# The first input of a two-layer trunk: transposed raw, in four blocks between the first weights, with its norm applied to the products

## The chip, the cores and the metric

One Trainium2 chip, one of its cores. The metric is the device time of one execution in microseconds (us); lower is better. The kernel before has a median of 2629.19 us over three runs (2629.15 to 2630.71). TensorE is called PE here, VectorE DVE, ScalarE ACT, GpSimd POOL and SyncE SP, as the profile does.

## The reference

Two layers over 256 tokens of 2048 channels, in float32: a gated DeltaNet mixer and then an attention over picked tokens, each followed by a squared-ReLU MLP. Each part starts with an RMS norm. What matters here is the beginning:

```
def rms_norm(x, g):
    y = xf * lax.rsqrt(jnp.mean(xf * xf, axis=-1, keepdims=True) + EPS)
    return y * g
...
u = rms_norm(h, norm_mix[0])            # h is the input x, [256, 2048]
proj = u @ w_in                         # [2048, 12352]: q, k, v, z, b, a
qkv = silu(causal_conv(qkv, conv_w))
beta = sigmoid(b); g = -exp(a_log) * softplus(a + dt_bias)
o = chunk_gated_delta_rule(l2norm(q), l2norm(k), v, g, beta)
o = rms_norm(o, out_norm) * silu(z)
h = h + o @ w_out
h = h + square(relu(rms_norm(h) @ w_up)) @ w_down
```

The norm multiplies each token (a row of x) by one number, 1/sqrt(mean + eps), and each channel by a gain. The number of the token can as well be applied to the product `proj`, token by token. The convolution, its SiLU, the sigmoid, the softplus and the SiLU of z come after it.

## The kernel before

**Products.** All large products run on PE as three products of float32r parts: each operand a is split into `hi` (a rounded copy) and `lo` (the rest), and hi·hi + hi·lo + lo·hi is summed (`mm3`). `x` stands transposed, [128 channels, 256 tokens] for each of 16 blocks k of 128 channels, as `xhi` and `xlo`. The weights come through `Stream`: a tile `raw` of 128 x 1024 is loaded by SP, ACT writes `whi` (a cast), DVE writes `wlo` (raw minus whi). There are four buffers each for `raw`, `whi` and `wlo`; an item of the first layer holds two blocks k. The split runs three items ahead of the products, so the cast of item i+3 can only start when PE has finished with item i-1.

**Order.** Nothing is scheduled behind the program's back: each engine runs its instructions in the order in which the Python code emits them. `Pace` keeps a rough account of when each engine will be free, and `Background` uses it to emit the steps of side chains (generators) between the blocks of the main work: `tick` emits those that should be due, `ensure` emits steps until a named result is there. `by_channel` and `by_token` are the two loops of products; `by_channel` calls `ensure` for block k + `ahead` before it emits the products of block k.

**DMA.** A load that SP or ACT issues signals one of eight completion semaphores, handed out in turn; an issue that reuses one waits until the load before on it has landed, and everything behind it on that engine waits as well.

**The start** (lines 384 to 452). SP loads x in four quarters, then the identity `ident` (part of the tile `wide`), then eight small vectors of gains into `rows`, then the first weights. ACT and DVE square the quarters (`junk`), DVE sums and takes the reciprocal root (`rsqrt`, ten small steps), PE transposes `rows` into `vecs`, and `normalise(c)` scales 512 columns of x. The generator `first` transposes a block of x on PE (two matmuls with `ident` into a bank `aux`) and splits it into `xhi` (ACT) and `xlo` (DVE), with the gain of the channel. Two blocks are emitted ahead; then group 0 of the projections starts with `ahead=3`: 16 blocks, 12 products each, into two banks `acc`.

**Layer 0** (lines 454 to 725). After group 0 come the products of b and a (48), the chain `decays` (DVE, ACT, then a transpose of the tile `E` on PE), and the products of z (`zo`). For each of 16 groups of two heads, ACT copies the four products of [128, 256] into `s`, and the chain `delta` does the convolution, the triangular inverse and the output `r`, in the background of the next groups' products.

Of the kernel before, what the change touches and what calls it, by code (L numbers as in the profile page):

```python
# [27 lines left out]
class Pace:  # L28
    """A rough account of when each engine gets through what it has been given, in microseconds."""
# [98 lines left out]
class Stream:  # L128
    """The weights in the order of their use: loaded, and split into two float32r parts, ahead of it."""
# [9 lines left out]

    def get(self):  # L140
# [3 lines left out]
        while self.split < min(i + ahead + 1, len(self.items)) or self.loaded < min(i + self.loads + 1, len(self.items)):  # L144
            while self.loaded < min(self.split + self.loads - self.ahead, len(self.items)):
                (n, w), pieces = self.items[self.loaded]
                raw = self.raw_pool.tile([P, 1024], F32, name="raw")
                view = raw[:, : n * w].rearrange("p (n w) -> p n w", n=n)
                for at, src in pieces:
                    self.sync.dma_start(out=at(view), in_=src)  # L150
                self.raw[self.loaded] = raw
                self.loaded += 1
# [17 lines left out]
def tile_hybrid_trunk(ctx: ExitStack, tc: tile.TileContext, a: dict, out: bass.AP):  # L170
# [38 lines left out]
    QO, KO, VO, ZO, BO = 0, 2048, 4096, 8192, 12288  # L209
    for g in range(DN_G):  # L210
        for k in range(0, KD, 2):
            ws.add((2, 512), [
# [68 lines left out]
    def rsqrt(y, x, n, eng=dve):  # L281
        """y = 1/sqrt(x), elementwise over [P, n]."""
# [14 lines left out]
    def split(src, hi, lo, scale=None):  # L297
        """float32 values in PSUM or SBUF, scaled by the partition, as two float32r parts."""
# [42 lines left out]
    def by_channel(n_items, part, key, n_ct=4, ahead=0):  # L341
        """Channels on partitions: [128 channels, 256 tokens] each, two to a bank."""
# [16 lines left out]
    def by_token(n_items, part, key, n_cols=512, outs=None, k0=0):  # L359
        """Tokens on partitions: [128 tokens, n_cols] for each of the two blocks of tokens."""  # L360
# [17 lines left out]
    def two_chunks(tiles, key, nk):  # L378
        """The first two blocks of columns of a mixer's output, which leave the last heads to the end."""
        outs = [by_token(nk // 2 - 2, h_part(tiles), key) for _ in range(2)]  # L380
        return [by_token(2, h_part(tiles), key, outs=o, k0=nk - 4) for o in outs]

# [1 line left out]
    with tc.tile_pool(name="first", bufs=1) as fp:  # L384
# [3 lines left out]
        quarters = [(tb, slice(c * 1024, c * 1024 + 1024)) for c in range(2) for tb in range(2)]  # L388
        for tb, s in quarters:
            sync.dma_start(out=xin[:, tb, s], in_=a["x"][0, tb * P:tb * P + P, s])  # L390
        sync.dma_start(out=ident, in_=a["consts"][:, 0:P])
        dve.memset(rows, 0.0)
        at = 0
        VEC = {}
        for name, src in (
# [4 lines left out]
            sync.dma_start(out=rows[at:at + n, :], in_=src.rearrange("(n p) -> n p", p=P))  # L400
# [9 lines left out]
        sq4 = small_tile(4, "sq4")  # L410
        for n, (tb, s) in enumerate(quarters):
            junk = fp.tile([P, 1024], F32, name="junk", bufs=2)
            if n % 2 == 0:
                act.activation(junk, xin[:, tb, s], AF.Square, accum_out=sq4[:, n:n + 1])
            else:
                dve.scalar_tensor_tensor(junk, xin[:, tb, s], 1.0, xin[:, tb, s], op0=OP.mult, op1=OP.mult, accum_out=sq4[:, n:n + 1])
        rs = small_tile(2, "rs")
        sq = small_tile(2, "sq")
        dve.tensor_tensor(sq, sq4[:, 0:2], sq4[:, 2:4], op=OP.add)
        dve.tensor_scalar(sq, sq, 1.0 / D, EPS, op0=OP.mult, op1=OP.add)  # L420
        rsqrt(rs, sq, 2)
# [4 lines left out]
        def normalise(c):  # L426
            s = slice(c * 512, c * 512 + 512)
            act.activation(xin[:, 0, s], xin[:, 0, s], AF.Copy, scale=rs[:, 0:1])
            dve.tensor_scalar(xin[:, 1, s], xin[:, 1, s], rs[:, 1:2], None, op0=OP.mult)

        normalise(0)

        def first():
            for k in range(KD):
# [5 lines left out]
                if k % 4 == 1 and k < 12:  # L440
                    normalise(k // 4 + 1)
                yield
            t = aux()
            for i in range(2):
                pe.transpose(t[:, i * P:i * P + P], cwr[:, i, :], ident)
            act.copy(cw, t[:, 0:T])

# [3 lines left out]
        first_banks = by_channel(8, x_part, "x0", ahead=3)  # L451
        bg.drain()

# [1 line left out]
    tokc = const.tile([P, 2, P], F32, name="tokc")  # L455
    GLM, BETA, GL = 32, 64, 96
    hT = []
    with tc.tile_pool(name="delta", bufs=2, reuse_waits="tile") as dp:
        gl_dram = dramp.tile([DN_H, T], F32, name="gl_dram")

        def decays(ps):
# [6 lines left out]
            act.activation(ba[64:96], ps[64:96, :T], AF.Tanh, scale=0.5)  # L468
# [3 lines left out]
            dve.tensor_scalar(xa, ps[q, :T], par[q, 1:2], None, op0=OP.add)  # L472
# [28 lines left out]
        def delta(g, s, zg):  # L501
# [86 lines left out]
            # (1 + L)^-1 by doubling its diagonal blocks. L^T is la[b][:, i, 0]; of the four matrices the blocks of 32 are  # L588
            # held apart, T in Tc and T^T in Tct, until they are put together in Tt
# [58 lines left out]
            # y = T r, with what the first block takes from the second's r  # L648
# [17 lines left out]
            # o, its norm and its gate  # L666
# [21 lines left out]
            pool.tensor_tensor(pair(f), pair(f), rep(sc), op=OP.mult)  # L688
            yield True
# [13 lines left out]
        for g in range(DN_G):  # L703
# [4 lines left out]
            for c in range(2):  # L708
                act.copy(s[:, 2 * c:2 * c + 2].rearrange("p n t -> p (n t)"), banks[c])
# [6 lines left out]
            for b in range(2):  # L716
                act.activation(zg[:, b], zo[b], AF.Tanh, scale=0.5)
# [8 lines left out]

    spare[:] = [None, "pk0", None, "pk1"]

# [6 lines left out]
    def chunk_done(outs, c, key, gain, scale=None, last=True):  # L735
        """A block of 512 columns of the residual stream; where it is final, what the next layer takes."""
# [62 lines left out]
    with tc.tile_pool(name="dsa", bufs=1, reuse_waits="tile") as sp, ExitStack() as late:  # L799
# [15 lines left out]
        def q_latent():  # L815
            # 1/sqrt(mean(q^2) + eps) of q = rstd*u is rsqrt(mean(u^2) + eps/rstd^2)/rstd
# [228 lines left out]
```

## Time and profile before

| what | value |
|---|---|
| median of three runs | 2629.19 us (2629.15 to 2630.71) |
| span of the profiled execution (first to last instruction) | 2626.4 us |
| its own device time | not listed apart; the fastest run is 2629.15 us, 2.8 us above the span |
| PE busy | 2588.8 us, 99% |
| DVE, ACT, POOL busy | 1546.4 us (59%), 1292.3 us (49%), 331.1 us (13%) |
| first x transpose, first product, third product | 15.15, 18.38, 19.64 us |
| DMA | 455.95 MB, mean 174 GB/s |

Busy time is the union of an engine's instructions; a matmul's end is modelled, so neighbouring matmuls overlap in the rows, and the step from one start to the next says more than the duration. "Line 78" is the helper through which every compute instruction is emitted, so tiles, not lines, tell what an instruction is. Times are counted from the span's start. A wait names what ended last before the instruction; where that engine had long been done, it was another, often a DMA.

### The profile page before, as it was taken

The page shows a single profiled execution, that of the slowest core. Times are in us where ns is not written, and L with a number is a line of the kernel's source. Part 1 is how long each engine was busy: PE and PEld are TensorE (multiplying, and loading weights), DVE is VectorE, ACT ScalarE, POOL GpSimd, SP SyncE. Part 2 cuts the span into 40 slices and gives each one's busy share as a digit, 9 for nine tenths or more (in the row PEclk, how much of TensorE's full clock was granted, in tenths as well). Part 3 has the DMA queues.
Part 4 walks back from the last instruction along what each step waited for, and adds up shares of the span by engine and source line. Part 5 has one row for each costly group of instructions (what it writes and reads, how often), then busy time and mean ns, then how long its engine had stood idle before and what let it go on. Part 6 is the DMA issues. An engine that isn't in the chain of part 4 may idle for free.

```text
span 2626.4 us, 52946 instructions
## 1 busy us (share of the span) xinstructions
PE 2588.8 (99%) x21827; PEld 2362.0 (90%) x21827; DVE 1546.4 (59%) x2313; ACT 1292.3 (49%) x1995; POOL 331.1 (13%) x674
## 2 busy tenths in 40 slices
PE   7999999999999999999999999999999999999997
PEld 7999999999987899988899988898899988999886
DVE  5777676676764555554455554586555544455544
ACT  4555555555554444443344444566544433444443
POOL 0344444343431000000000000000000000000000
PEclk9999999999999999999999999999999999999999
DMA  6655455555554566666666666643666666666664
GB/s 191 186 147 141 137 150 139 149 146 147 144 168 153 182 189 195 194 193 193 193 186 186 190 190 188 181 133 120 179 191 194 193 195 194 189 188 187 192 193 137
DMA packets 325394, 455.95 MB, mean 174 GB/s; under 512 B 18280, under 2 KB 159840, under 8 KB 324768
## 3 DMA queue, kind: packets, MB, share of 16 engines
q1 hardware_dynamic: 321888, 443.85, 56.8%
q10 hardware_dynamic: 2928, 7.37, 0.8%
q8 instruction: 171, 2.80, 0.4%
q0 software_dynamic: 336, 1.34, 0.1%
q14 instruction: 71, 0.58, 0.1%
HBM read 450.37 MB, written 2.13 MB: 172 GB/s over the span
## 4 chain that ended last, share of the span: by engine, by line
PE 66%; DVE 1%; ACT 0%; issue 0%; ACTq 0%; DVEq 0%
PE acc L78 64%; PE aux L78 1%; PE pk L78 1%; DVE wlo L78 0%; DVE score L78 0%; ACT whi L78 0%; DVE p L78 0%; DVE m L78 0%; ACT acc L78 0%; DVE qtl L78 0%; DVE nm L78 0%; ACT h L78 0%; DVE h L78 0%; DVE rs_t L78 0%; DVE rs_u L78 0%
## 5 line engine op out<-in xcount | busy, mean ns | idle before, releaser
L78 DVE TENSOR_TENSOR wlo<-raw,whi 128x1024 fp32r<-128x1024 f32 x842 | 1029.6, 1229 | 868.4 <-ACT whi L78 861.3
L78 ACT CAST whi<-raw 128x1024 fp32r<-128x1024 f32 x842 | 878.3, 1049 | 853.3 <-PE acc L78 820.7
L78 PE MATMUL acc<-whi,h 128*128 128x512 f32 x2816 | 886.0, 392 | 2.1 <-ACT acc L78 2.1
L78 PE MATMUL acc<-xhi,whi 128*128 128x256 f32 x3088 | 875.9, 284 | 0.3 <-ACT whi L78 0.3
L78 PE MATMUL acc<-xhi,wlo 128*128 128x256 f32 x3088 | 860.5, 279 | 0.5 <-DVE wlo L78 0.5
L78 PE MATMUL acc<-xlo,whi 128*128 128x256 f32 x3088 | 860.8, 279 | 0.0
L78 PEld LDWEIGHTS acc<-whi,h 128*128 128x128 f32 x2816 | 528.7, 188 | 112.2 <-ACT acc L78 2.9
L78 PEld LDWEIGHTS acc<-xhi,wlo 128*128 128x128 f32 x3088 | 585.1, 189 | 0.8 <-DVE wlo L78 0.8
L78 PEld LDWEIGHTS acc<-xhi,whi 128*128 128x128 f32 x3088 | 581.3, 188 | 4.6 <-ACT whi L78 0.7
L78 PEld LDWEIGHTS acc<-xlo,whi 128*128 128x128 f32 x3088 | 581.8, 188 | 0.2
L78 PE MATMUL acc<-wlo,h 128*128 128x512 f32 x1408 | 548.3, 389 | 0.0
L78 PEld LDWEIGHTS acc<-wlo,h 128*128 128x128 f32 x1408 | 264.5, 188 | 52.7
L78 PE MATMUL acc<-whi,xhi 128*128 128x256 f32 (+2 forms) x576 | 173.6, 301 | 0.0
L78 PE MATMUL acc<-whi,xlo 128*128 128x256 f32 (+2 forms) x576 | 166.4, 289 | 0.0
L78 PE MATMUL acc<-wlo,xhi 128*128 128x256 f32 (+2 forms) x576 | 166.1, 288 | 0.0
L78 POOL DMA_DIRECT2D gain<-in_norm_final x1 | 0.6, 639 | 973.2 <-issue 973.2
L78 DVE SCALAR_TENSOR_TENSOR y<-s,cw,y 128x255 f32<-128x255 f32 (+2 forms) x192 | 93.8, 489 | 40.5 <-ACT y L78 36.0
L78 POOL TENSOR_SCALAR E<-R,tokc 128x128 f32<-128x128 f32 x96 | 86.3, 911 | 247.6 <-DMA R<-gl_dram 144.7
L78 PEld LDWEIGHTS acc<-whi,xhi 128*128 128x128 f32 x576 | 108.0, 187 | 3.6
L78 POOL TENSOR_TENSOR h<-h,gain 128x512 f32<-128x512 f32 x8 | 10.1, 1283 | 790.5 <-ACT acc L78 790.5
L78 PEld LDWEIGHTS acc<-wlo,xhi 128*128 128x128 f32 x576 | 108.3, 188 | 1.3
L78 PEld LDWEIGHTS acc<-whi,xlo 128*128 128x128 f32 x576 | 108.1, 188 | 1.2
(239 smaller groups left out, 1955.9 us busy)
## 6 DMA issues: line engine op xcount, KB each, us to landing
raw<-in_mlp_w_up SPq DMA_DIRECT2D x256, 512.0 KB, 4.3
raw<-in_mlp_w_down SPq DMA_DIRECT2D x256, 512.0 KB, 4.3
raw<-in_dn_w_in SPq DMA_DIRECT2D x66, 512.0 KB, 4.1
raw<-in_dn_w_in SPq DMA_DIRECT2D x256, 128.0 KB, 2.9
raw<-in_dn_w_in SPq DMA_DIRECT2D x128, 256.0 KB, 3.3
raw<-in_dn_w_out SPq DMA_DIRECT2D x64, 512.0 KB, 3.8
raw<-in_dsa_w_out SPq DMA_DIRECT2D x32, 512.0 KB, 3.7
raw<-in_dsa_w_uq SPq DMA_DIRECT2D x16, 512.0 KB, 4.2
```

What stands on the lines that cost most here:

```text
L78: r = f(*args, **kwargs)
```

## The change

x comes in four blocks of 512 columns for all tokens, each listed as a piece of a weight item (items 0, 2, 4 and 6), so that SP issues it between the weights. The identity and the gains are loaded from ACT's queue. PE begins with ten matmuls of the tile `ones` with itself. `first` transposes and splits raw x; the squares of a block follow its fourth transpose, and after block 15 come the reciprocal root `rs0` [128, 2], two diagonal tiles `dg`, and a matmul of ones with them that writes the root as a row over all partitions, `rs_row` [128, 256]. `by_channel` for group 0 gets `ahead=1`. What was normalised before is now scaled behind the products: `s` (DVE instead of ACT), the two inputs of `decays`, the tanh of z (scale `rs_half`), and one more POOL multiplication in the output's factor `f`.

```
@@ Stream
+    def fetch(self):
+        while self.loaded < min(self.split + self.loads - self.ahead, len(self.items)):
...
@@ the list of weights, group 0
+            block = slice(k * P, k * P + 512)
+            ws.add((2, 512), ([((lambda v, c=block: xin[:, :, c]), x_rows[:, :, block])] if g == 0 and k % 4 == 0 else []) + [
...
@@ the start
-        quarters = [(tb, slice(c * 1024, c * 1024 + 1024)) for c in range(2) for tb in range(2)]
-        for tb, s in quarters:
-            sync.dma_start(out=xin[:, tb, s], in_=a["x"][0, tb * P:tb * P + P, s])
-        sync.dma_start(out=ident, in_=a["consts"][:, 0:P])
+        t = aux()
+        for _ in range(10):
+            pe.matmul(t[:, 0:P], lhsT=ones, rhs=ones, start=True, stop=True)
         dve.memset(rows, 0.0)
+        act.dma_start(out=ident, in_=a["consts"][:, 0:P])
...
-            sync.dma_start(out=rows[at:at + n, :], in_=src.rearrange("(n p) -> n p", p=P))
+            act.dma_start(out=rows[at:at + n, :], in_=src.rearrange("(n p) -> n p", p=P))
...
-        normalise(0)
+        def squares(c):
+            s = slice(c * 512, c * 512 + 512)
+            junk = fp.tile([P, 2, 512], F32, name="junk", bufs=2)
+            act.activation(junk[:, 0], xin[:, 0, s], AF.Square, accum_out=sq8[:, c:c + 1])
+            dve.scalar_tensor_tensor(junk[:, 1], xin[:, 1, s], 1.0, xin[:, 1, s], op0=OP.mult, op1=OP.mult,
+                                     accum_out=sq8[:, 4 + c:5 + c])
@@ first
                 split(t[:, :T], xT[0][:, k], xT[1][:, k], vec("mix0", k))
                 ready.add(("x0", k))
-                if k % 4 == 1 and k < 12:
-                    normalise(k // 4 + 1)
-                yield
+                yield
+                if k % 4 == 3:
+                    squares(k // 4)
+            sq = small_tile(2, "sq")
+            dve.tensor_reduce(sq, sq8.rearrange("p (b c) -> p b c", b=2), axis=AX.X, op=OP.add)
+            dve.tensor_scalar(sq, sq, 1.0 / D, EPS, op0=OP.mult, op1=OP.add)
+            rsqrt(rs0, sq, 2)
+            dg = fp.tile([P, 2, P], F32, name="dg")
+            for tb in range(2):
+                dve.tensor_scalar(dg[:, tb], ident, rs0[:, tb:tb + 1], None, op0=OP.mult)
+            yield
+            t = aux()
+            pe.matmul(t[:, :T], lhsT=ones, rhs=dg.rearrange("p b c -> p (b c)"), start=True, stop=True)
+            act.copy(rs_row, t[:, :T])
+            yield
...
-        first_banks = by_channel(8, x_part, "x0", ahead=3)
+        first_banks = by_channel(8, x_part, "x0", ahead=1)
@@ decays
-            act.activation(ba[64:96], ps[64:96, :T], AF.Tanh, scale=0.5)
+            dve.tensor_tensor(ba[64:96], ps[64:96, :T], rs_row[64:96], op=OP.mult)
+            act.activation(ba[64:96], ba[64:96], AF.Tanh, scale=0.5)
...
-            dve.tensor_scalar(xa, ps[q, :T], par[q, 1:2], None, op0=OP.add)
+            dve.tensor_tensor(xa, ps[q, :T], rs_row[q], op=OP.mult)
+            dve.tensor_scalar(xa, xa, par[q, 1:2], None, op0=OP.add)
@@ delta, the output's factor
+            pool.tensor_tensor(pair(f), pair(f), rep(rs0), op=OP.mult)
@@ the groups
-                act.copy(s[:, 2 * c:2 * c + 2].rearrange("p n t -> p (n t)"), banks[c])
+                dve.tensor_tensor(s[:, 2 * c:2 * c + 2], banks[c].rearrange("p (n t) -> p n t", n=2),
+                                  rs_row.unsqueeze(1).to_broadcast([P, 2, T]), op=OP.mult)
...
-                act.activation(zg[:, b], zo[b], AF.Tanh, scale=0.5)
+                act.activation(zg[:, b], zo[b], AF.Tanh, scale=rs_half[:, b:b + 1])
```

How the order on the engines moves is seen at three places. The first is ACT in the middle of group 0, before: `xhi` is the rounded part of a block of x, `whi` that of a weight item, `xin` the scaling of raw x.

```order
13 L78 CAST whi<-raw 128x1024 x2
14 L78 ACTIVATE xhi<-aux,vecs 128x256 x2
15 L78 CAST whi<-raw 128x1024
16 L78 ACTIVATE xhi<-aux,vecs 128x256
17 L78 ACTIVATE xin<-xin,rs 128x512
18 L78 ACTIVATE xhi<-aux,vecs 128x256
19 L78 CAST whi<-raw 128x1024
20 L78 ACTIVATE xhi<-aux,vecs 128x256 x2
```

The same stretch of ACT in the changed kernel, where `junk` holds the squares:

```order
19 L78 CAST whi<-raw 128x1024 x2
20 L78 ACTIVATE xhi<-aux,vecs 128x256 x2
21 L78 CAST whi<-raw 128x1024
22 L78 ACTIVATE xhi<-aux,vecs 128x256
23 L78 ACTIVATE junk,sq_131<-xin 128x512
24 L78 ACTIVATE xhi<-aux,vecs 128x256
25 L78 CAST whi<-raw 128x1024
26 L78 ACTIVATE xhi<-aux,vecs 128x256 x2
```

The pattern of casts and splits is the same, but counted from the start of the list there stand nine `xhi` ahead of row 15 before (blocks 0 to 8) and seven ahead of row 21 now (blocks 0 to 6). The cast there is that of item 6 in both, so the split of x runs two blocks less ahead of the weights. DVE has the same order with `xlo` and `wlo`.

The second place is the start of PE, first before:

```order
1 L78 MATMUL aux<-wide,rows 128x128
2 L78 MATMUL aux<-wide,xin 128x128 x8
3 L78 MATMUL acc<-xhi,whi 128x256
4 L78 MATMUL acc<-xlo,whi 128x256
5 L78 MATMUL acc<-xhi,wlo 128x256
```

and in the changed kernel:

```order
1 L78 MATMUL aux<-ones 128x128 x10
2 L78 MATMUL aux<-wide,rows 128x128
3 L78 MATMUL aux<-wide,xin 128x128 x4
4 L78 MATMUL acc<-xhi,whi 128x256
5 L78 MATMUL acc<-xlo,whi 128x256
6 L78 MATMUL acc<-xhi,wlo 128x256
```

Ten matmuls on ones stand ahead of everything, and two blocks of x (four transposes) instead of four stand ahead of the first product.

The third place is PE at the end of group 0 in the changed kernel; `dg` is the diagonal tile of the root, `cwr` the raw weights of the convolution, and the products from row 212 on are those of `decays`.

```order
207 L78 MATMUL acc<-xhi,whi 128x256
208 L78 MATMUL acc<-xlo,whi 128x256
209 L78 MATMUL acc<-xhi,wlo 128x256
210 L78 MATMUL aux<-dg,ones 128x256
211 L78 MATMUL aux<-wide,cwr 128x128 x2
212 L78 MATMUL acc<-xhi,whi 128x256
213 L78 MATMUL acc<-xlo,whi 128x256
```

Before, the transposes of `cwr` stand two blocks earlier, between the products of blocks 13 and 14, and no matmul waits for a norm. Now the matmul with `dg` stands behind the last product of group 0 and ahead of all later ones.

## Rows read from the trace of the kernel before

**Rows 1.** The page's span and its first section: busy time of each engine.
```profile
span 2626.4 us, 52946 instructions
PE 2588.8 (99%) x21827; PEld 2362.0 (90%) x21827; DVE 1546.4 (59%) x2313; ACT 1292.3 (49%) x1995; POOL 331.1 (13%) x674
```
**Rows 2.** What PE waited for, whole span: total us, times, longest us.
```profile
PE aux L78 <- DVE sq L78: 12.3, 1, 12.3
PE aux L78 <- ACT xin L78: 2.4, 1, 2.4
PE acc L78 <- ACT acc L78: 2.1, 2, 1.0
...
PE aux L78 <- DVE E L78: 1.5, 1, 1.5
```
**Rows 3.** Timeline of the start: start us, duration us, engine, instruction, idle before.
```profile
11.62 0.08 DVE L78 DVE_READ_ACCUMULATOR junk<-xin 128x1 f32 x1
...
12.31 0.45 PE L78 MATMUL aux<-wide,rows 128*128 128x128 f32 x1 [12.31 <-DVE sq L78]
...
14.18 0.16 DVE L78 SCALAR_TENSOR_TENSOR rs<-rs_u,rs 128x2 f32<-128x2 f32 x1
...
15.15 1.11 PE L78 MATMUL aux<-wide,xin 128*128 128x128 f32 x4 [2.40 <-ACT xin L78]
...
18.38 0.58 PE L78 MATMUL acc<-xhi,whi 128*128 128x256 f32 x1 [0.28 <-ACT whi L78]
...
19.64 0.58 PE L78 MATMUL acc<-xhi,wlo 128*128 128x256 f32 x1 [0.47 <-DVE wlo L78]
```
**Rows 4.** Timeline of the start: the first landing of x, the last small load.
```profile
5.38 1.06 ACT L78 ACTIVATE junk<-xin 128x1024 f32<-128x1024 f32 x1 [3.37 <-DMA xin<-in_x]
...
10.66 0.25 SPq L400 DMA_DIRECT2D rows<-in_dn_out_norm  x1
```
**Rows 5.** Timeline of PE in group 0: steps early and late.
```profile
23.86 0.41 PE L78 MATMUL acc<-xlo,whi 128*128 128x256 f32 x1
24.07 0.41 PE L78 MATMUL acc<-xhi,wlo 128*128 128x256 f32 x1
...
39.22 0.38 PE L78 MATMUL aux<-wide,xin 128*128 128x128 f32 x2
...
40.84 0.38 PE L78 MATMUL aux<-wide,xin 128*128 128x128 f32 x2
```
**Rows 6.** Busy time by stretch: length, engines (instructions), granted clock, DMA share, GB/s.
```profile
15.00:24.30 9.30, 7.69 (x32) 6.49 (x33) 5.16 (x9) 5.87 (x11) 0.00 (x0) 1.00 0.89 243
24.50:46.70 22.20, 22.20 (x195) 22.20 (x195) 15.52 (x22) 14.14 (x23) 0.00 (x0) 1.00 0.71 197
...
77.40:120.00 42.60, 42.19 (x469) 40.91 (x470) 35.60 (x65) 25.54 (x42) 20.68 (x29) 1.00 0.66 183
120.00:740.00 620.00, 619.71 (x8648) 585.10 (x8647) 436.16 (x929) 355.86 (x758) 265.84 (x555) 1.00 0.52 143
```
**Rows 7.** Timeline of PE: first product after group 0; f32 matmuls of 768 columns.
```profile
46.75 0.28 PE L78 MATMUL acc<-xhi,whi 128*128 128x256 f32 x1
...
94.06 1.45 PE L78 MATMUL pk<-s 128*128 128x512 f32 x4
```
**Rows 8.** Timeline of ACT and DVE: a cast, its rest, the next split of x.
```profile
31.22 1.05 ACT L78 CAST whi<-raw 128x1024 fp32r<-128x1024 f32 x1 [0.79 <-PE acc L78]
...
32.30 1.23 DVE L78 TENSOR_TENSOR wlo<-raw,whi 128x1024 fp32r<-128x1024 f32 x1 [0.94 <-ACT whi L78]
33.44 0.48 DVE L78 SCALAR_TENSOR_TENSOR xlo<-aux,vecs,xhi 128x256 fp32r<-128x256 f32 x1
```
**Rows 9.** Groups by form: out, in, count, busy us, mean ns, idle before.
```profile
L78 DVE TENSOR_TENSOR h<-acc,h 128x512 f32<-128x512 f32 x16 | 10.1, 682 | 0.0
...
L78 ACT COPY s<-acc 128x512 f32<-128x512 f32 x26 | 14.1, 591 | 1.3 <-PE acc L78 1.1
```
**Rows 10.** Timeline of PE: the transposes of E in the chain of decays.
```profile
77.45 0.44 PE L78 MATMUL aux<-wide,E 128*128 128x128 f32 x2 [1.49 <-DVE E L78]
```

More of the change, by code (lines that the diff above doesn't have):

```diff
@@ L138, in add @@
         self.items.append((shape, pieces))
+    def fetch(self):
+        while self.loaded < min(self.split + self.loads - self.ahead, len(self.items)):
+            (n, w), pieces = self.items[self.loaded]
+            raw = self.raw_pool.tile([P, 1024], F32, name="raw")
+            view = raw[:, : n * w].rearrange("p (n w) -> p n w", n=n)
+            for at, src in pieces:
+                self.sync.dma_start(out=at(view), in_=src)
+            self.raw[self.loaded] = raw
+            self.loaded += 1
     def get(self):
@@ L144, in get @@
         while self.split < min(i + ahead + 1, len(self.items)) or self.loaded < min(i + self.loads + 1, len(self.items)):
[L145 to L152, printed above, removed]
+            self.fetch()
             if self.split >= min(i + ahead + 1, len(self.items)):
@@ L209, in tile_hybrid_trunk @@
     QO, KO, VO, ZO, BO = 0, 2048, 4096, 8192, 12288
+    x_rows = a["x"][0].rearrange("(b p) d -> p b d", p=P)
     for g in range(DN_G):
         for k in range(0, KD, 2):
-            ws.add((2, 512), [
+            block = slice(k * P, k * P + 512)
+            ws.add((2, 512), ([((lambda v, c=block: xin[:, :, c]), x_rows[:, :, block])] if g == 0 and k % 4 == 0 else []) + [
                 (lambda v: v[:, :, 0:128], w_in[:, k:k + 2, KO + g * 128:KO + g * 128 + 128]),
@@ L381, in two_chunks @@
         return [by_token(2, h_part(tiles), key, outs=o, k0=nk - 4) for o in outs]
+    carry = ExitStack()
+    carried = carry.enter_context(tc.tile_pool(name="carried", bufs=1))
+    tokc = carried.tile([P, 2, P], F32, name="tokc")
+    rs0 = carried.tile([P, 2], F32, name="rs0")
+    rs_half = carried.tile([P, 2], F32, name="rs_half")
+    rs_row = carried.tile([P, T], F32, name="rs_row")
     with tc.tile_pool(name="first", bufs=1) as fp:
@@ L408, in vec @@
             return vecs[:, VEC[name] + i:VEC[name] + i + 1]
[L410 to L421, printed above, removed]
+        sq8 = small_tile(8, "sq8")
+        ws.fetch()
         tp = aux()
@@ L424, in tile_hybrid_trunk @@
         act.copy(vecs, tp[:, 0:72])
-        def normalise(c):
+        def squares(c):
             s = slice(c * 512, c * 512 + 512)
-            act.activation(xin[:, 0, s], xin[:, 0, s], AF.Copy, scale=rs[:, 0:1])
-            dve.tensor_scalar(xin[:, 1, s], xin[:, 1, s], rs[:, 1:2], None, op0=OP.mult)
-        normalise(0)
+            junk = fp.tile([P, 2, 512], F32, name="junk", bufs=2)
+            act.activation(junk[:, 0], xin[:, 0, s], AF.Square, accum_out=sq8[:, c:c + 1])
+            dve.scalar_tensor_tensor(junk[:, 1], xin[:, 1, s], 1.0, xin[:, 1, s], op0=OP.mult, op1=OP.mult,
+                                     accum_out=sq8[:, 4 + c:5 + c])
         def first():
@@ L446, in first @@
             act.copy(cw, t[:, 0:T])
+            ready.add("first")
         bg.add(first())
@@ L450, in tile_hybrid_trunk @@
         bg.step()
-        first_banks = by_channel(8, x_part, "x0", ahead=3)
+        first_banks = by_channel(8, x_part, "x0", ahead=1)
         bg.drain()
-    tokc = const.tile([P, 2, P], F32, name="tokc")
     GLM, BETA, GL = 32, 64, 96
@@ L459, in tile_hybrid_trunk @@
         gl_dram = dramp.tile([DN_H, T], F32, name="gl_dram")
+        dve.tensor_scalar(rs_half, rs0, 0.5, None, op0=OP.mult)
         def decays(ps):
@@ L725, in tile_hybrid_trunk @@
         bg.drain()
+    carry.close()
     spare[:] = [None, "pk0", None, "pk1"]
```

## The prediction, made before the result was known

> **What bounds the kernel now.** I read the page's first section, then the list of what TensorE waited for, then the start of the timeline, then the busy time by stretch. The page says that TensorE (PE) is the bound: it is busy for 2588.8 of 2626.4 us [rows 1]. So a change is worth only what it takes from the 37.6 us in which PE does not work, or what it adds to them. The list of waits shows where these are: 12.3 + 2.4 us lie ahead of the first products, and the next ones are 2.1 us and 1.5 us [rows 2]. Everything that the change can win lies therefore in the first 20 us. What it can lose lies anywhere in layer 0, whose order it alters.
>
> The start goes like this [rows 3]. PE transposes the parameter rows at 12.31, then waits. VectorE (DVE) ends the squares of the raw input at 11.62, takes until 14.34 for the reciprocal root, the first quarter is scaled, PE transposes from 15.15, and the first product starts at 18.38; its third product must wait for `wlo` until 19.64. The first block of x had landed by 5.38, the last small load was issued at 10.66 [rows 4]. So the products start 13 us after the first half MB is there, and that chain is what the change cuts.
>
> From there PE runs without a gap. [...] The 192 products of group 0 end there: the one that starts at 46.75 is the first of the next stage, `decays` [rows 7]. That is the point at which I compare.
>
> **The change part by part.** *The start.* The squares, the root and the scaling no longer stand ahead of the first transposes. What still does: the parameter rows, because the split of x takes its gains from them. They now come from ScalarE's (ACT's) queue, nine issues, of which the last four wait for earlier loads to land. These loads and SP's share eight completion semaphores, so that an issue waits until an earlier load has landed, as the one at 10.66 did before. The trace has no such queue at the start. Bounds for the transpose of the rows: not before x could land, 5.4 [rows 4], and not after its old 12.31. I take 8.2, nearer to 5.4, because SP keeps at most some 0.8 MB in flight instead of 2 MB. From that transpose to the first product it was 0.45 us to its end, and 3.23 from the x transposes to the product, 0.6 of it a scaling that now goes: 8.2 + 0.45 + 2.65 = 11.3. Call this S; it is 7.1 us earlier than 18.38. From the bounds, S lies between 8.5 and 15.4.
>
> *The run after S.* 192 products at 0.1135 are 21.8 us and 14 pairs of transposes at 0.26 are 3.6: 25.4. The third product waits for `wlo` as before: 1.0 us. Then comes a price. `ahead` falls from 3 to 1, so the order puts the transposes of block k+2 between the products of k and k+1. ACT and DVE stay in order: for each pair of blocks the split of the next-but-two weight tile stands between the two splits of x (the order's rows in the part on the change). That `whi` waits until PE has done with its buffer, i.e. until the products of an odd block end. Before, it went: `whi` 31.22, `wlo` 32.30, `xlo` 33.44 to 33.92 [rows 8], 2.7 us from the release to `xlo`, plus 0.1 to PE. Before, three blocks of products lay in that time. Now PE has one pair of transposes, 12 products, another pair and one product: 0.26 + 1.36 + 0.26 + 0.11 = 1.99 us, and then stands for 0.85. This comes at blocks 7, 9, 11, 13 and 15: 4.3 us. At blocks 3 and 5 two weight tiles stand in a row ahead of the split; walking the same durations gives 1.1 and 0.85. Sum of stalls: 6.3 us.
>
> *The end of group 0.* The norm now comes last: after the last `xlo` DVE does the squares of 512 columns (about 0.65, half of the old 1024), the root (2.7 us from 11.62 to 14.34, [rows 3]) and two diagonal tiles (0.4): 3.75 us. PE has 11 products left, 1.25 us, and the matmul of ones with the diagonal stands next in its order, ahead of the whole next stage: 2.5 us of wait. The matmul itself is 256 columns of f32; 768 take 1.45 us [rows 7], so 0.45; with the conv transposes 0.7.
>
> *Clock.* Before, PE stepped at 0.21 for 6.0 us after its first product, though it had been working on and off since 15.15. [...] So I take the low level again until S + 6.0. Slow products cost less than before, since the stalls shrink beneath them (at 0.21 the chain of 2.8 us hides under 12 products of 2.56): walking it, 1.4 us against a start at the high level.
>
> [...]
>
> *Sum to the comparison point:* 11.3 + 25.4 + 1.0 + 6.3 + 2.5 + 0.7 + 1.4 = 48.6, against 46.75: 1.9 us later. A start that is 7 us earlier is spent on 6.3 of new stalls, 3.2 of the late norm, and little else.
>
> *Layer 0 after that.* `s` is now a DVE multiply from PSUM, 0.68 us, where ACT copied in 0.59 [rows 9]: 32 of them, 1.36 us of DVE per group. DVE is busy for 436 of 620 us between 120 and 740, and PE is never idle there; but between 77.4 and 120 DVE is at 84% [rows 6]. I cost this at 0 where cover is 30% and 0.4 us in the dense stretch; the bound above is the whole 1.36 in 15 groups, 20 us, and below nothing, since ACT was not what PE waited for. `decays` has two more DVE steps (about 1 us) ahead of the transposes of E, for which PE waited 1.5 us [rows 10]; these now stand 12 products (1.36 us) later in PE's order: -0.4. One more GpSimd step of four columns per group lies behind other work. Sum 0.
>
> The profile's span is 2626.4; the runs' median of 2629.2 lies 2.8 above it, which I leave as it is, since the change lies inside the span. Forecast: 2629.2 + 1.9 = 2631.1, i.e. **no change that a measurement of this kernel can tell** (0.2%, 5.3 us, is about that bound).
>
> **The rivals.**
> - *The clock is up at S* (the ones do it, or the idle stretch does not undo it). For: ten dense matmuls. Against: the 6 us of [rows 5] after work since 15.15. Time: 2629.7. Chance 22%.
> - *The lost look-ahead costs nothing*, because ACT and DVE run the splits of x before PE needs them. For: before, DVE waited for `whi`, not for work. Against: the in-order chain of 2.7 us in [rows 8]. Then -6.3 us: 2624.8, with the clock up as well 2623.4, the only way past -0.2%. Chance 12%.
> - *DVE becomes the bound in layer 0* (the slower side): `s` stands in DVE's order ahead of the weights' `wlo`, and PE runs out of split weights. It decides once more than about half of the 1.36 us per group is exposed: 0.6 × 15 = 9 us, 2640. For: 84% in the dense stretch. Against: 30% idle later, and `wlo` waits mostly for buffers. Chance 10%.
> - *The rows land no earlier* because of the shared semaphores: S = 15.4, 4.1 us more: 2635.2; from there anything above makes it measurably slower. Chance 11%.
>
> **How the numbers follow.** The forecast has 45%, the rivals the rest. Measurably faster: most of the stall-free case with something else going well, and an S near 8.5 with the clock up (-2.3): 11%. Measurably slower: the DVE case and half of the late-rows case: 16%. The rest, 73%, is within 0.2%. The range goes from the stall-free case, 2624.5, to just beyond the late rows, 2637.
>
> **What would show it.** First product between 9.5 and 13, not 18.4. In group 0, waits of PE for `xlo` of 0.8 to 1.1 us at every second block, about 6 us in all, and one of about 2.5 us for `dg`; if they are missing, the second rival holds. The stage after group 0 starting at 47 to 49. The step of the first products (0.21 or 0.114) tells the clock. PE idle of under 2 us more than before between 60 and 780; if it is 5 or more, with DVE named, the third rival holds. A first product after 14 means the fourth. Wrong is this prediction if the time falls below 2624 or exceeds 2637, or if it falls between them with the start and the stalls both absent.

## The result, and the profile after

The changed kernel takes 2646.74 us (median of 4 runs, 2645.53 to 2648.14), the kernel before 2629.17 (4 runs, 2629.05 to 2630.71). The ratio is 1.0065, 95% interval 1.0051 to 1.0078: it is slower by 0.65%, 17.6 us. The forecast was 2631.1, range 2624.5 to 2637, so the time lies outside the range. The profiled execution has a span of 2646.0 us, 19.6 more than before. It is the slowest of the four (2648.14 us); their mean granted clock goes from 0.995 (this one) to 0.998 (2645.53 us), so what the clock takes in this trace need not come in every execution.

The page's first section, after (answers to [rows 1]):
```profile
span 2646.0 us, 53033 instructions
PE 2610.2 (99%) x21849; PEld 2382.1 (90%) x21849; DVE 1574.4 (60%) x2350; ACT 1279.7 (48%) x1964; POOL 331.8 (13%) x690
```
TensorE (PE) idles for 35.8 us, where it was 37.6. It is the *busy* time that grew, by 21.4 us, for 22 matmul records more (the ten products of ones and the one with `dg`, two records each). Some 4 us of it cost nothing, since the ones run while PE had nothing else to do:
```profile
1.05 4.05 PE L78 MATMUL aux<-ones 128*128 128x128 f32 x20 [1.05 <-DVE ones L78]
```
A share of busy time doesn't say how long a matmul takes.

The list of PE's waits, after (total us, times, longest us; answers to [rows 2, 10]):
```profile
PE acc L78 <- DVE xlo L78: 4.6, 7, 0.9
PE aux L78 <- DMA rows<-in_dn_out_norm: 4.4, 1, 4.4
PE aux L78 <- DVE rs_half L78: 2.3, 1, 2.3
...
PE aux L78 <- DVE E L78: 0.5, 1, 0.5
```
The 12.3 us for `sq` are gone; 4.4 for the parameter rows, 4.6 for `xlo` and 2.3 for the norm (the wait named `rs_half`) have come.

The timeline of PE at the start, after (answers to [rows 3]):
```profile
9.53 0.45 PE L78 MATMUL aux<-wide,rows 128*128 128x128 f32 x1 [4.43 <-DMA rows<-in_dn_out_norm]
9.77 1.21 PE L78 MATMUL aux<-wide,xin 128*128 128x128 f32 x4
12.47 0.58 PE L78 MATMUL acc<-xhi,whi 128*128 128x256 f32 x1 [1.50 <-ACT whi L78]
```
And inside group 0 (answers to [rows 5]):
```profile
28.23 0.38 PE L78 MATMUL aux<-wide,xin 128*128 128x128 f32 x2
28.37 0.36 PE L78 MATMUL acc<-xhi,whi 128*128 128x256 f32 x1
29.43 0.39 PE L78 MATMUL acc<-xlo,whi 128*128 128x256 f32 x1 [0.70 <-DVE xlo L78]
...
30.84 0.38 PE L78 MATMUL aux<-wide,xin 128*128 128x128 f32 x2
32.48 0.38 PE L78 MATMUL aux<-wide,xin 128*128 128x128 f32 x2
```
Between two pairs of transposes lie 2.61 us where `xlo` is awaited (28.23 to 30.84) and 1.64 where it is not (30.84 to 32.48): 0.97 us a stall, near the forecast's walk (0.85). There are five such stalls, one smaller (0.24 us of idle) and, before the last block, one larger (0.90).

The timeline of PE at the end of group 0, after (answers to [rows 7]: the product at 51.52 is the first of `decays`; the one at 59.07 is the first of the gate's, `zo`):
```profile
50.26 1.19 PE L78 MATMUL aux<-dg,ones 128*128 128x256 f32 x2 [2.29 <-DVE rs_half L78]
51.24 0.63 PE L78 MATMUL aux<-wide,cwr 128*128 128x128 f32 x2
51.52 0.56 PE L78 MATMUL acc<-xhi,whi 128*128 128x256 f32 x1
51.88 0.41 PE L78 MATMUL acc<-xlo,whi 128*128 128x256 f32 x1
...
55.66 0.28 PE L78 MATMUL acc<-xlo,whi 128*128 128x256 f32 x1
55.77 0.28 PE L78 MATMUL acc<-xhi,wlo 128*128 128x256 f32 x1
...
59.07 0.28 PE L78 MATMUL acc<-whi,xhi 128*128 128x256 f32 x1
```
After the wait of 2.29 us the clock is at its low level again: the products step at 0.21 us from 51.88 on (granted clock 0.56 in 52:56) and at 0.11 or 0.12 only from 55.66 (1.00 in 56:60). The 48 products of `decays` take 7.55 us (51.52 to 59.07); before, they took 5.44, from 46.75 to the first product of the gate:
```profile
52.19 0.28 PE L78 MATMUL acc<-whi,xhi 128*128 128x256 f32 x1
```

Busy time by stretch, after (length, then busy us and instructions of PE, PEld, DVE, ACT, POOL, then granted clock, DMA share, GB/s; answers to [rows 6]):
```profile
0.00:11.00 11.00, 5.50 (x25) 4.66 (x25) 0.31 (x2) 1.97 (x3) 3.22 (x9) 0.85 0.73 207
11.00:24.00 13.00, 10.83 (x69) 10.34 (x70) 9.28 (x13) 8.56 (x13) 0.00 (x0) 0.73 1.04 317
...
48.00:80.00 32.00, 29.75 (x230) 29.49 (x231) 21.61 (x40) 12.65 (x17) 0.00 (x0) 0.89 0.45 123
...
160.00:760.00 600.00, 600.00 (x8331) 565.07 (x8333) 447.18 (x928) 336.29 (x704) 250.48 (x544) 1.00 0.53 148
```
Here the granted clock shows the level: 0.85 in the first 11 us (it rose near the end of the ones, whose step falls from 0.21 to 0.11 us at about 4.4, and fell again before the first product: it reads 0.50 from 8 to 18 us, where the products step at 0.21), 0.73 in the next stretch, and 0.89 after the wait. In layer 0 PE is busy for 600.00 of 600 us, and the changed kernel doesn't fall further behind there: 6.9 us at the first product of the gate (59.07 against 52.19), 5.5 at the end. The DVE multiplies cost nothing.

I then took the time at which each of the 842 weight tiles is cast, in both traces, and subtracted. The changed kernel is 5.5 us behind when layer 0 ends, 12.3 us behind after the first half of MLP 0 (its 1536 products of the up projection), still 13 at the second MLP's start, and 19.6 after the first up half of MLP 1. So some 13 us are lost in two stretches in which the change alters no instruction. One view shows it: PE's matmuls in 100 us of each of the four up halves (stretch, its length, PE's busy time and count, granted clock, DMA share, GB/s). Before:
```profile
1000.00:1100.00 100.00, 100.00 (x885) 1.00 0.65 200
1350.00:1450.00 100.00, 100.00 (x852) 1.00 0.63 193
1960.00:2060.00 100.00, 100.00 (x885) 1.00 0.65 200
2310.00:2410.00 100.00, 100.00 (x851) 1.00 0.62 194
```
After:
```profile
1000.00:1100.00 100.00, 100.00 (x851) 1.00 0.59 182
1350.00:1450.00 100.00, 100.00 (x852) 1.00 0.61 185
1960.00:2060.00 100.00, 100.00 (x852) 1.00 0.61 188
```
PE is busy for every one of the 100 us, at full clock, in all of them. But before, the first halves run 885 products (113 ns each), the second halves 852 (117.4 ns); after, all run at 117.4. 1536 products × 4.4 ns = 6.7 us a half, 13.5 in all. I call the two levels the 113 and the 118 ns step.

### The profile page after: what moved, and what is told of

It reads as the page before. It is cut to its first block, busy times and chain, and to the rows that moved or that the text cites. A ratio compares the mean times of both kernels' runs of the same rounds, so it can differ in the third digit from the quotient of the medians.

```text
span 2646.0 us, 53033 instructions
## 1 busy us (share of the span) xinstructions
PE 2610.2 (99%) x21849; PEld 2382.1 (90%) x21849; DVE 1574.4 (60%) x2350; ACT 1279.7 (48%) x1964; POOL 331.8 (13%) x690
## 4 chain that ended last, share of the span: by engine, by line
PE 93%; DVE 3%; DMA 1%; ACT 1%; issue 1%; POOL 1%; SPq 0%; ACTq 0%; DVEq 0%; POOLq 0%
PE acc L78 84%; PE aux L78 7%; PE pk L78 2%; DVE wlo L78 2%; DMA raw<-in_dn_w_in 1%; ACT whi L78 1%; DMA R<-gl_dram 0%; DVE y L78 0%; POOL rs_u L78 0%; SPq L146 0%; POOL f L78 0%; DVE score L78 0%; POOL E L78 0%; DMA wide<-in_consts 0%; DVE p L78 0%
```

## Experiments

"a_" is an edit of the changed kernel, "b_" one of the kernel before. Times are medians of 4 to 10 executions in three rounds, beside the kernel before on the same chip (2628.4 to 2630.0), ratios to that with 95% intervals. "Place" means an address in an SBUF partition, given as what it lies over a multiple of 256 bytes. The up projection loads `whi` or `wlo` as the stationary operand and streams `xhi` or `xlo`. Before, the weights' tiles have place 32 and the x tiles 224; in the changed kernel `tokc` has left the constants for a pool of its own, every weight tile lies 896 bytes lower, at place 160, and x stays at 224.

**1. The weights' addresses, put back (a_pad) and taken over (b_shift).**
```diff
-    tokc = carried.tile([P, 2, P], F32, name="tokc")
+    tokc = const.tile([P, 2, P], F32, name="tokc")
...
-        sq8 = small_tile(8, "sq8")
+        sq8 = fp.tile([P, 8], F32, name="sq8")
```


> The changed kernel with two small tiles put elsewhere in SBUF, so that raw, whi, wlo and h have the addresses that they have in the kernel before; no instruction is added or moved. Theory A (the addresses set the product step): the first up half of both MLPs falls from 118 to 113 ns a step, 1536 products x 4.4 ns = 6.7 us each, and the time from 2646.7 to about 2633. Theory B (the step is set by what PE ran before it, not by addresses): both stay at 118 ns and the time within 1 us of 2646.7.

2633.69 us, ratio 1.0018 (1.0009 to 1.0028). Its up halves of MLP 0:
```profile
1000.00:1100.00 100.00, 100.00 (x884) 1.00 0.62 194
1350.00:1450.00 100.00, 100.00 (x852) 1.00 0.59 186
```
The reverse, on the kernel before (`tokc` in a pool that closes after layer 0, 128 bytes of padding, so that the addresses are the changed kernel's):
```diff
-    tokc = const.tile([P, 2, P], F32, name="tokc")
+    carried = carry.enter_context(tc.tile_pool(name="carried", bufs=1))
+    tokc = carried.tile([P, 2, P], F32, name="tokc")
...
+    pad = const.tile([P, 32], F32, name="pad")
```


> The kernel before with tokc put elsewhere, so that raw, whi, wlo and h have the addresses of the changed kernel; no instruction of TensorE is added or moved. Theory A (addresses): the first up half of both MLPs goes from 113 to 118 ns and the time from 2629.2 to about 2642. Theory B (what PE ran before): 113 ns stays, 2629 stays.

2642.14 us, ratio 1.0049 (1.0034 to 1.0064), 852 matmuls in 100 us in the first halves. Theory A holds in both directions and in size: 13.05 us come back (12.7 if each time is set against the kernel before beside it), 13.3 are lost, and PE's instructions are the same. Of the 17.6 us, 13 are where `tokc` lies.

**2. The ones on the kernel before (b_ones).** The ten products are put ahead of its first transpose.

> The kernel before with the ten products of ones ahead of its first transpose and nothing else. Theory B (PE's history sets the step): the step of the first up halves may turn to 118 ns, +6.7 us for each; theory A (addresses): they stay at 113 ns. For the start: the ten products raise the clock to full by about 5 us as in the changed kernel (0.85 granted over 0:11), and it is back at half before the first product at 18.4, so that the start gains nothing: 46.7 for the first decays product, within 0.3 us.

2629.16 us, ratio 1.0001 (0.9991 to 1.0010); 885 matmuls in the first halves. What PE ran at the start doesn't set the step (what it runs just before the products can, see 6), and the ones gain nothing.

**3. The look-ahead (a_ahead3).**
```diff
-        first_banks = by_channel(8, x_part, "x0", ahead=1)
+        first_banks = by_channel(8, x_part, "x0", ahead=3)
```


> The changed kernel with the look-ahead of the transposes at 3 blocks, as before, in place of 1. Theory C (the look-ahead costs its stalls): the PE waits for xlo, 4.6 us over seven places, go to under 0.5, and the first decays product comes 2 to 4.6 us earlier than 51.9; the wait for dg grows by what the chain of the norm doesn't gain. Rival: the wait at dg takes all of it (grows from 2.3 to 6 or more) and the stage ends at 51.9 as now. The MLP step says the rest: 6.7 us for each first up half that turns to 113 ns (theory B allows it, theory A doesn't).

2636.89 us, ratio 1.0030 (1.0019 to 1.0042): 9.85 us less than the changed kernel. Its waits in the first 110 us:
```profile
PE aux L78 <- DMA rows<-in_dn_out_norm: 3.6, 1, 3.6
PE aux L78 <- DVE E L78: 1.5, 1, 1.5
...
PE aux L78 <- DVE dg L78: 0.7, 1, 0.7
PE aux L78 <- DVE xlo L78: 0.6, 1, 0.6
```
and by stretch, as above:
```profile
24.00:48.00 24.00, 23.34 (x198) 23.06 (x198) 17.49 (x40) 12.57 (x21) 0.00 (x0) 1.00 0.65 184
48.00:80.00 32.00, 30.52 (x268) 30.32 (x267) 26.00 (x43) 14.13 (x20) 0.46 (x1) 1.00 0.59 174
```
The first `decays` product comes at 41.57, where it was 51.52: 9.95 us earlier, twice what theory C, which counted the idle time of the stalls alone, expected. The stalls cost 6.5 us with the time lost behind each (five of 0.97; the other two, by the same rows, some 0.5 and 1.2). With the transposes done earlier the norm is done earlier as well, and the wait falls from 2.3 to 0.7 us. The product with `dg` and its transposes take 0.65 us (40.92 to 41.57) in place of 1.26, since the clock stays up: the products behind it step at 0.12 us, and the column says 1.00 in 48:80, where it was 0.89. The rest, some 1.3 us, is in the start: the first product 0.3 us earlier, two pairs of transposes ahead of it and not behind, and the full step from 16.8 us on in place of 18.1. The step in the MLPs is 118 ns as theory A says (852 in 100 us). The rival, that the wait for `dg` eats the gain, is refuted.

**4. The wait for the norm, moved behind `decays` (a_lateg).**
```diff
         first_banks = by_channel(8, x_part, "x0", ahead=1)
+        first_ba = by_channel(2, x_part, "x0", n_ct=1)[0]
         bg.drain()
...
-                bg.add(decays(by_channel(2, x_part, "x0", n_ct=1)[0]))
+                bg.add(decays(first_ba))
```


> The changed kernel with the 48 decays products emitted ahead of the wait for the norm: the product of ones with dg now comes near the end of them in place of ahead of them. Theory D (the wait for dg costs twice, once as idle 2.3 us and once more as 6.8 us in which the clock is at half, some 3.4 us): the wait for dg goes, the clock stays full from 18 us on, and the time falls by 5 to 6 us, to about 2641. Rival (the drop of the clock comes from the product of ones in fp32 or from the stalls on xlo, not from this wait): only 2.3 us, to 2644.4, with the clock still at half after 48 us.

2644.76 us, ratio 1.0062 (1.0047 to 1.0077): 2.0 us less than the changed kernel, not 5 to 6. The intervals of the two overlap, and the two profiled spans (2644.7 and 2646.0) differ by 1.3, so a gain this small isn't clear of the noise. Its waits and stretches:
```profile
PE aux L78 <- DVE E L78: 2.2, 1, 2.2
```
```profile
48.00:80.00 32.00, 32.00 (x273) 31.95 (x272) 23.01 (x39) 13.58 (x19) 0.00 (x0) 1.00 0.59 168
80.00:96.00 16.00, 13.78 (x106) 13.58 (x105) 14.26 (x26) 6.30 (x9) 4.88 (x6) 0.89 0.58 162
```
The first part of theory D came true: no wait for `dg`, full clock in 48:80, and the first gate product at 53.74, where it was 59.07, 5.3 us earlier. Then PE ran ahead of the chain that leads to `E`, waited 2.2 us there (0.5 in the changed kernel), and the clock fell after that wait: the wait ends at 85.88, the step goes from 0.12 to 0.21 us at 87.0, and the granted clock is 0.89 over the 16 us of 80:96, 1.7 us lost. 5.3 - 1.7 - 1.7 = 1.9. Most of the gain went into the next wait; the rival's total was near by accident: it wanted the clock still at half after 48 us, and there it is full.

**5. Both repairs (a_pad_ahead3), and the same without the ones (a_noones).** The edits of a_pad and a_ahead3 together:

> Both repairs of the changed kernel at once: the weights' tiles at the addresses of before, and the look-ahead of 3. If the two effects are separate they add: 2646.7 - 13.0 - 9.9 = 2623.8, that is some 5 us under the kernel before (ratio 0.998). Rival: the look-ahead's gain came in part through the step (113 or 118 ns) in layer 0, and the sum is 2626 to 2629, no faster than before.

2623.33 us, ratio 0.9979 (0.9969 to 0.9989). The two effects add (2623.8 expected), and the changed kernel's idea is then worth 5 us over the kernel before. Without the ones:

> The changed kernel with the look-ahead of 3 and the weights at the addresses of before, without the ten products of ones. If they bring the clock up sooner, full clock comes later than 17.4 us without them, and the time rises by half of the delay (each us at half clock costs 0.5): 2624 to 2626.5. Rival (the clock follows the transposes and products from 9 us on, and the ones are over too early): full at 17 to 18 us and 2623.3 as with them.

2623.15 us, ratio 0.9978 (0.9968 to 0.9988): the time that the rival named (2623.3). The ones are worth nothing at the start.

**6. Turning the step (b_flip).**
```diff
             for p in range(8):
+                if half == 1 and p == 1:
+                    t = aux()
+                    for tb in range(2):
+                        pe.transpose(t[:, tb * P:tb * P + P], h[:, tb, 0:P], ident)
                 banks = by_channel(8, x_part, key)
```


> The kernel before with one pair of transposes more (not used for anything) at the second of the eight column blocks of each second up half. Theory E (at these addresses the products can run at either step, and a pair of transposes between them takes them from 118 to 113 ns, where they stay): the second halves run at 113 ns from there on, 1344 products x 4.4 ns = 5.9 us each, and the time falls from 2628.8 to about 2617. Rival (the second halves are at 118 ns for another reason, such as what other engines do then): 118 ns throughout, 2629.

2616.87 us, ratio 0.9957 (0.9942 to 0.9972). Two stretches of the second halves, and PE's matmuls in 20 us on either side of the first pair, which stands at 1320.41:
```profile
1350.00:1450.00 100.00, 100.00 (x885) 1.00 0.65 200
...
2310.00:2410.00 100.00, 100.00 (x885) 1.00 0.62 190
```
```profile
1300.00:1320.00 20.00, 20.00 (x172) 1.00 0.67 194
1330.00:1350.00 20.00, 20.00 (x179) 1.00 0.59 176
```
At the places of before the products can run at either step; they keep the one they have for over a thousand products (the gain, 2628.45 to 2616.87, is two halves of some 1300 products at 4.4 ns), and one pair of transposes takes them from 118 to 113 ns. In the first half of MLP 0 of the kernel before, the transposes of the normed input between the first blocks do that: twelve products take 1.42 us ahead of the first pair (948.96 to 950.38), 118 ns each, and nine steps 1.02 us behind it (950.85 to 951.87), 113 ns each. The second halves have no transposes. In the changed kernel the same pairs stand in the first halves, and the step stays at 118 ns.

**7. Which place counts (b_pad128, b_padw, b_pad256, b_padx).** Padding ahead of the weights' tiles in the kernel before, of 128 bytes (ahead of `raw`):
```diff
+    pad = const.tile([P, 32], F32, name="pad")
```


> The kernel before with 128 bytes a partition left empty ahead of the weights' tiles, so that raw, whi, wlo and h move up by 128 bytes; TensorE's instructions are the same. Theory A in its narrow form (the place within 256 bytes counts: 32 over a multiple in before, 160 over in the changed kernel and here): first up halves at 118 ns, about 2642. Rival (what counts is a coarser position, or the distance to the moving operand in a larger unit): 113 ns stays, 2629.

2639.82 us, ratio 1.0045 (1.0030 to 1.0060), 852 matmuls: 128 empty bytes cost 11.4 us. The same between `raw` and `whi`:

> The kernel before with the 128 empty bytes between raw and whi, so that raw stays and whi, wlo and the tiles of h behind them move. Theory A for the weights that TensorE loads: first up halves at 118 ns, about 2640 as with the pad ahead of raw. Rival (the address of raw counts, which the transfers write and ScalarE and VectorE read): 113 ns stays, 2628.5.

2640.96 us, ratio 1.0048 (1.0033 to 1.0063), 852: it isn't `raw`, but the tiles behind the pad; x, the residual stream and the identity that the transposes read stay. With 256 bytes:

> The kernel before with 256 empty bytes ahead of raw. If places repeat every 256 bytes, as 128 bytes turning 113 to 118 ns suggest, the first up halves are back at 113 ns and the time at 2628.5; if any move from the place of before turns them, 118 ns and about 2640.

2629.17 us, ratio 1.0004 (0.9994 to 1.0013), 884: a move as such costs nothing. And x moved by 128 bytes in the MLPs, the weights left:
```diff
         stack = ExitStack()
+        if hT:
+            pad = stack.enter_context(tc.tile_pool(name="padp", bufs=1, side="right")).tile([P, 32], F32, name="pad")
         pool = stack.enter_context(tc.tile_pool(name="xtp", bufs=1, side="right", reuse_waits="tile"))
```


> The kernel before with the other operand moved: in both MLPs the transposed input xhi and xlo lie 128 bytes lower, the weights stay. If the step hangs on the distance between stationary and moving operand, the first up halves go to 118 ns (2640); if it hangs on the place of the weights alone, they stay at 113 ns (2628.5).

2643.45 us, ratio 1.0057 (1.0042 to 1.0072), 851 matmuls in the first halves. I took this for proof that the distance between the operands counts. It isn't, as the next run shows.

**8. The distance theory, tried (a_padx), and two more pairs of places (b_al256, b_x64).** The edit of b_padx on the changed kernel: weights at 160, x at 96, the distance of before up to a multiple of 256 bytes.

> The changed kernel with the weights left where it puts them (160 bytes over a multiple of 256) and, in both MLPs, xhi and xlo 128 bytes lower, so that the distance between the two operands is that of the kernel before again, though neither is at its address. If the distance counts: first up halves back at 113 ns, 2646.7 - 13 = about 2633.5. If it is the address of either that counts: 118 ns, 2646 to 2647.

2646.70 us, ratio 1.0067 (1.0052 to 1.0082). Its first up half:
```profile
1000.00:1100.00 100.00, 100.00 (x851) 1.00 0.59 183
```
The distance theory falls: the same distance, 118 ns. Of the other two, b_al256 has 224 bytes of padding ahead of the weights and 224 below x in the first MLP:

> The kernel before with the weights' tiles on multiples of 256 bytes (224 bytes up) and x in the first MLP on a multiple of 256 too (224 down), in the second MLP where it was (224 over). Theory F (operands that begin on a multiple of 256 can take the short step): first up half of the first MLP at 113 ns, of the second perhaps; time 2629 to 2636. Rival (only the pair of before, 32 and 224 over, takes it): 118 ns in both, 2641.

2658.63 us, ratio 1.0110 (1.0095 to 1.0125); 28.6 us more than the kernel before beside it. The counts of its four up halves (836, 835, 848 and 847 in 100 us, for 885, 852, 885 and 851) give an estimate of 22 of them, at 1536 products each; where the other 6 lie is not shown. First halves of its two MLPs:
```profile
1000.00:1100.00 100.00, 100.00 (x836) 1.00 0.59 183
...
1960.00:2060.00 100.00, 100.00 (x848) 1.00 0.62 191
```
b_x64 has 64 and 32 bytes below x in the first and second MLP:

> The kernel before with x 64 bytes lower in the first MLP (160 over a multiple of 256) and 32 bytes lower in the second (192 over), weights as before. If the place counts in steps of 128 bytes only, both first up halves stay at 113 ns, 2629; if in steps of 64, the first turns to 118 ns and the second stays, 2635; if in steps of 32, both turn, 2641.

2653.07 us, ratio 1.0088 (1.0071 to 1.0105), 836 and 845 matmuls. Both times are longer than any that was expected: there are worse steps (100 us / 836 = 119.6 ns), operands on multiples of 256 bytes have one of them, and 32 bytes already matter. Here the second halves are slower too (835 in 100 us in the first MLP, where it was 852).

**9. All together (a_turn).** The edits of a_pad and a_ahead3, and a pair of transposes after the first block of each second up half:
```diff
+                if turn and k == 0:
+                    t = aux()
+                    for tb in range(2):
+                        pe.transpose(t[:, tb * P:tb * P + P], h[:, tb, 0:P], ident)
```


> The changed kernel with the weights at the addresses of before, the look-ahead of 3, and a pair of transposes more (not used for anything) after the first block of each second up half, which takes the products to 113 ns there. The effects add: 2623.3 - 2 x 6.7 + 0.6 = 2610.5, ratio 0.993. Rival: at the first block, so soon after the products of the first down half, the pair doesn't turn the step, and the time stays at 2623 to 2624.

2611.59 us, ratio 0.9936 (0.9919 to 0.9953), the fastest of all: 17 us under the kernel before and 35 under the changed one. All four up halves run at 113 ns:
```profile
1000.00:1100.00 100.00, 100.00 (x885) 1.00 0.64 196
1350.00:1450.00 100.00, 100.00 (x885) 1.00 0.64 195
```

## Why the prediction was wrong

*The premise failed.* "So a change is worth only what it takes from the 37.6 us in which PE does not work, or what it adds to them", and "What it can lose lies anywhere in layer 0". Both leave PE's busy time outside layer 0 as it was: this is the step that failed. The idle time even fell, by 1.8 us; the busy time rose. The move of `tokc` was part of the change and got no term in the sum, as it adds no instruction. It is worth 13.0 of the 17.6 us (a_pad, and b_shift from the other side): 3072 products of the two first up halves step at 118 ns in place of 113.

*The start was mis-sized by 2.9 us, with most of its mechanism right.* Sum to the first `decays` product: 48.6 forecast, 51.52 measured, 46.75 before. By its terms, 1.2 + 1.4 - 0.2 + 0.6 within rounding:
- The first product: 11.3 forecast, 12.47 measured; the transpose of the rows came at 9.53, not 8.2. ACT's last four issues of nine came late, as the forecast had it: the fifth at 2.75, then 4.83, 5.53, 6.76 and 7.10. Within the bounds (8.5 to 15.4), and no rival is borne out: the fourth wanted 15.4.
- Group 0 from there: 25.4 + 1.0 + 6.3 + 1.4 = 34.1 forecast, 35.5 measured (12.47 to 47.97, where the wait for the norm begins). The forecast's 0.1135 us a product and 0.26 a pair of transposes are those of [rows 5], 1.62 for twelve and a pair; where nothing is awaited 1.64 were measured (30.84 to 32.48). The stalls of the smaller look-ahead are 4.6 us of idle at seven places and cost 6.5: right, and the second rival (they cost nothing) is refuted by a_ahead3. Half of the 1.4 too much lies in the first two blocks, 6.10 us (12.47 to 18.57) where the forecast's terms give 5.4: the price of the low clock was too small.
- The late norm: 2.5 forecast, 2.29 measured. The product with `dg` and the conv transposes: 0.7 forecast, 1.26 measured, since they ran at the low clock.
- The clock at the start: low until S + 6.0 forecast; the steps change at about 18, S + 5.5. Right. The first rival (clock up at S) is refuted, the 0.85 in the first 11 us notwithstanding: what the ones raised was gone before the first product (0.50 granted from 8 to 18 us; the product starts at 12.47). The step falls from 0.21 to 0.12 us at about 18 under dense products and is 0.21 again at 51.88 behind a wait of 2.29.
- Not foreseen: this second fall of the clock, at the wait for the norm. Up to the point of comparison it costs the 0.6 us on the `dg` product and its transposes. Behind that point, and so not in the 2.9, it costs 2.1 us more on `decays` (7.55 against 5.44).

*Layer 0 after that*: 0 forecast, 2.1 us lost on `decays`. The wait for `E` shrank from 1.49 to 0.5 (forecast: by 0.4), PE has no idle time between 160 and 760, and the third rival (DVE becomes the bound) is refuted: DVE is busy for 447 of those 600 us and PE waits for nothing. 4.8 + 2.1 - 1.0 = 5.9 us; at the end of layer 0 the trace has 5.5.

Without the move of `tokc` the time is 2633.7 (a_pad), slower than before by 0.18%, inside the range and 2.6 us from the forecast. The walk through the start found what it walked through, but for the second fall of the clock; the large loss came from a place that it didn't look at.

## What to carry to other kernels

Where PE is busy all the time, count its matmuls per stretch in the profile before and after: here a busy share of 100% hid a step that had grown by 4% (113 to 117.4 ns), and a moved allocation caused it without one instruction being changed (b_pad128: 11.4 us). A pad of some bytes, or a pair of transposes that nobody uses, is then worth a run (b_flip: 11.6 us gained); a pad can also cost (b_al256: 28.6 us, b_x64: 23.1). A wait of PE is to be priced with the slow clock that may follow it, and a gain in front of a wait with what the next wait takes back (a_lateg: 3.4 of 5.3 us). Here the waits of 2.29 us (the changed kernel, 2.7 us lost behind it) and 2.22 (a_lateg, 1.7) were followed by the slow step; those of 0.90 (the changed kernel, 46.40) and 1.49 (the kernel before, 77.45) were not.

## What the runs showed of the hardware

- The 256-column products in fp32r step at 113, 118 or 120 ns at a granted clock of 1.00 (885, 852 and 836 in 100 us of the up halves), depending on where in SBUF their two operands lie. Weights/x by place: 32/224 gives 113 or 118, and holds what it has (the kernel before, b_flip); 160/224 (the changed kernel, b_shift, b_pad128), 32/96 (b_padx) and 160/96 (a_padx) gave 118 in all halves (851 or 852); 0/0 (b_al256) and 32/160 (b_x64) gave 120 (835 or 836); 0/224 and 32/192 (their second MLPs) gave some 118 (848 and 845). A move by 256 bytes changed nothing (b_pad256: 884, 2629.17 us). The rule is open: the distance alone is ruled out (a_padx), and why a pair of transposes turns the step wasn't found. The first halves have such pairs at every place tried and reach 113 only at 32/224; no run put one into a second half at another place.
- Both addresses count: b_padx moves the streamed operand alone (851 in 100 us for 885), b_padw the loaded one and not the streamed one (852), and with either each product takes 4 ns longer. In what way they count, no run shows.
- In the up halves, where each product has a weight load of its own, the shortest step measured is 113 ns.
- Ten fp32 products of ones raised the clock only near their end, and not in every execution: their 20 records take 4.05 us in the profiled run of the changed kernel, with a step of 0.21 us that falls to 0.11 at about 4.4, and 4.63 in that of a_ahead3, where it stays at 0.21. The granted-clock column reads 1.00 for the first 24 us of a_ahead3, though its products step at 0.21 us until 16.6; there the step tells the level, not the column.
```profile
1.05 4.63 PE L78 MATMUL aux<-ones 128*128 128x128 f32 x20 [1.05 <-DVE ones L78]
```
- In both profiled runs the first products run at the low clock (0.21 us a step from 14.11 to 15.82 in the changed kernel, from 13.82 to 15.54 in a_ahead3), and with or without the ones the time is the same (2623.33 and 2623.15).
